# A two-sequence decoder layer rewritten: token-major residual, two halves of 512 tokens per pass, norms and attention placed between dense matmuls

## The chip, the cores and the metric

The kernel runs as one program on the eight cores of one Trainium2 chip. Each core has the same weights and two of the sixteen prompt sequences, with four of the 32 sample rows. The cores do not exchange data. The metric is the device time of the slowest core in microseconds.

Executions come in two states. In the fast one all cores agree within about 1%; in the slow one the cores of one die (0 to 3 or 4 to 7), sometimes of both, run longer at a lower mean clock.

In the profiles PE is TensorE (PEld its weight loads), DVE is VectorE, ACT is ScalarE, POOL is GpSimd and SP is SyncE; a name with a q (POOLq, SPq) is the part of an engine that issues DMAs. The granted clock is the share of its full rate at which TensorE ran. A mixer is the stage between the two FFNs: projections, pooling, attention, gates and output. Residue order for a step of 4 or 16 means that tokens with the same remainder lie side by side.

## The reference, cut to what matters

Per layer, with 1024 channels, sequences of 2048 tokens and a hidden width of 2816:

```python
x = x + 0.5 * swiglu(rmsnorm(x, norm_ffn1), ffn1_gate, ffn1_up, ffn1_down)
h = rmsnorm(x, norm_mix)
z = h @ w_in            # u (512) | 3 groups x (q, k, v) x 4 heads x 64 | gate_pool | gate_attn
pool = pool_mix(u)      # trailing means over 2, 4, 8, 16 tokens, a linear map per 128 channels
attn = 3 groups of causal windows (128, step 1), (512, step 4), (2048, step 16), rotary q and k,
       merged by their softmax denominators
x = x + (sigmoid(gate_pool) * (pool @ w_pool_br) + sigmoid(gate_attn) * (attn @ w_attn_br)) @ w_o
x = x + 0.5 * swiglu(rmsnorm(x, norm_ffn2), ffn2_gate, ffn2_up, ffn2_down)
y = rmsnorm(x, norm_final)
```

The outputs are y, the last pooling rows, and the key and value windows of the prompt; and the same for the sample rows. The sample rows' windows are cache rows shifted by one: about 22 MB per core that are only copied from one place in DRAM to another.

## The kernel before

One pass takes 512 tokens, so a core makes eight passes. The residual x is kept with channels on the partitions (`xT`). Each stage is its own block: norm, FFN, mixer, norm, FFN, final norm. Norms square all of x on ACT and DVE, average over the partitions with a matmul against a constant, and only then scale:

```python
def norm(gi, seg, out_f32=None, next_func=None):
    for c in range(8):
        if c % 2 == 0:  act: hT[:, c] = Square(xT[:, c])
        else:           dve: hT[:, c] = xT[:, c] * xT[:, c]
    K.mmg(b, [(ps[b][:, 0:n], meanm[:], hT_[:, c, 0:n], {"rd": [hT_.r[c]]}) for c in range(8)], ...)
    act: rstd = Exp(-0.5 * Ln(ps + EPS))
    for c in range(8):  dve: hT[:, c] = xT[:, c] * gains[c] * rstd
```

(shortened; the first and last lines of its loops stand for whole calls.) Rotated keys of the two groups with steps 4 and 16 are put into residue order by ACT copies that write with a stride (the normed x is copied in the same way before the values are projected):

```python
if g == 1:
    return [(kT1[:, ab, base:base + 512].rearrange("p (r i) -> p i r", r=4), slice(0, T))]
v = kT2[:, ab, :].rearrange("p (r m) -> p m r", r=16)
...
act.op(lambda dst=dst, src=src: nc.scalar.copy(out=dst, in_=src), reads=[kf.r[ab_]], writes=kres)
```

Weights are fp32 in DRAM. In the first pass a software DMA casts each tile and writes a bf16 copy back; later passes read the copy, once for each 512 tokens:

```python
def wload(first_pass, slot, slot_ap, src_f32, scr_ap, scr_res, sem3, arena_bound):
    if first_pass:
        ...
        pool.dma(slot_ap, src_f32, sem3[0], writes=slot.r)
        sp.dma(scr_ap, slot_ap, sem3[1], reads=slot.r, writes=[scr_res])
    else:
        ...
        sp.dma(slot_ap, scr_ap, sem3[2], reads=[scr_res], writes=slot.r)
```

The softmax here doesn't subtract the row's maximum and nothing guards it: scores larger than these inputs give would overflow.

## Time and profile before

4201.22 us, median of three runs (4198.58 to 4201.73).

| | before |
|---|---|
| passes 0 to 7, us | 790, 474, 485, 518, 471, 472, 474, 479 |
| the same in pairs (two passes, 1024 tokens) | 1264, 1003, 943, 953 |
| TensorE busy | 3484.7 us, 83% |
| read from HBM | 481.65 MB |

A pass length is the distance between two ends of the final norm in the chain of waits. Of the page of the kernel before, here are the busy time (us, share, instructions), TensorE's busy tenths in forty equal slices, and the granted TensorE clock in tenths in the same slices:

```profile
PE 3484.7 (83%) x19775; PEld 1817.0 (43%) x19775; DVE 1314.8 (31%) x2151; ACT 1016.3 (24%) x1625; POOL 247.4 (6%) x287
...
PE   1857875898997889867898879988898979987898
...
PEclk6977687997798969988799987999799987998799
```

The dips in the last two lines come together: where TensorE waits, its clock halves too. There is one such dip every four or five slices, one a pass (a slice is 105 us). 83% busy therefore overstates what TensorE does: matmuls at half clock are counted as busy for twice as long.

### The profile page before, as it was taken

Reading aid. Unit: us, or ns where it says so; the run is one execution under the profiler, and the core shown is the slowest. Engines: PE = TensorE matmul, PEld = TensorE weight load, DVE = VectorE, ACT = ScalarE, POOL = GpSimd, SP = SyncE. Lnnn points to the kernel's source line nnn. Section 1 sums busy time; section 2 is a strip of 40 time slices with the busy share of each in tenths; the row PEclk is TensorE's granted clock in tenths of the full one; section 3 lists DMA queues with packets and bytes.
Section 4 is the critical chain, followed back from the end, with each engine's and each line's share of the span. In section 5 each row is a group of like instructions: output and inputs, shape, how many; then the busy total and the mean of one; then the engine's idle time right before and its main releaser. Section 6 shows DMA issues by size and latency. Waiting matters only on the chain.

```text
span 4186.3 us, 55101 instructions; the slowest of 8 cores (4148.3 to 4186.3 us)
## 1 busy us (share of the span) xinstructions
PE 3484.7 (83%) x19775; PEld 1817.0 (43%) x19775; DVE 1314.8 (31%) x2151; ACT 1016.3 (24%) x1625; POOL 247.4 (6%) x287
## 2 busy tenths in 40 slices
PE   1857875898997889867898879988898979987898
PEld 0325532445543364433644345443644445443643
DVE  1125130325313333314333153134333162233432
ACT  1123220214211232112421142122321152122321
POOL 1100020002000020000200001000200010000200
PEclk6977687997798969988799987999799987998799
DMA  7963199531436206382164614452063423542151
GB/s 131 204 140 65 40 201 201 151 113 60 149 121 184 93 14 210 115 192 71 38 204 129 160 58 128 147 167 91 21 206 120 135 63 109 161 146 85 37 180 58
DMA packets 210535, 512.59 MB, mean 122 GB/s; under 512 B 19038, under 2 KB 116598, under 8 KB 200668
## 3 DMA queue, kind: packets, MB, share of 16 engines
q1 hardware_dynamic: 108512, 413.49, 31.3%
q0 software_dynamic: 101760, 95.58, 14.8%
q8 instruction: 166, 2.72, 0.3%
q14 instruction: 97, 0.79, 0.1%
HBM read 481.65 MB, written 98.24 MB: 139 GB/s over the span
## 4 chain that ended last, share of the span: by engine, by line
PE 68%; DMA 9%; DVE 7%; ACT 7%; issue 5%; another core or an unknown queue 3%; DVEq 0%; SPq 0%; POOL 0%; ACTq 0%; POOLq 0%
PE ps L190 60%; PE ps L896 4%; ACT sb_mergedT L203 3%; PE ps L188 2%; DMA sb_w_29<-wu 2%; DMA sb_w_28<-wscr 2%; PE ps L922 1%; DVE sb_xT L427 1%; DVE sb_hT L423 1%; DVE sb_qT L554 1%; DMA sb_w_33<-wu 1%; DMA sb_w_31<-wu 1%; DVE sb_hT L411 1%; DMA sb_w_28<-wg 1%
## 5 line engine op out<-in xcount | busy, mean ns | idle before, releaser
L190 PE MATMUL ps<-sb_hT,sb_w_30 128*128 128x512 bf16 x1152 | 304.8, 403 | 64.2 <-ACT sb_uext L662 36.1
L190 PE MATMUL ps<-sb_hT,sb_w_28 128*128 128x512 bf16 x768 | 210.4, 411 | 135.8 <-DMA sb_w_28<-wscr 58.2
L190 PE MATMUL ps<-sb_hT,sb_w_34 128*128 128x512 bf16 x1024 | 278.6, 412 | 26.6 <-DVE sb_hT L423 19.5
L190 PE MATMUL ps<-sb_hT,sb_w_31 128*128 128x512 bf16 x1152 | 285.6, 394 | 10.7 <-DMA sb_w_31<-wu 8.2
L190 PE MATMUL ps<-sb_hT,sb_w_35 128*128 128x512 bf16 x1024 | 242.9, 381 | 6.7 <-DMA sb_w_35<-wu 6.6
L190 PE MATMUL ps<-sb_hT,sb_w_29 128*128 128x512 bf16 x768 | 197.8, 406 | 57.2 <-DMA sb_w_29<-wu 57.2
L190 PE MATMUL ps<-sb_hT,sb_w_33 128*128 128x512 bf16 x896 | 212.5, 382 | 5.6 <-DMA sb_w_33<-wu 5.6
L190 PEld LDWEIGHTS ps<-sb_hT,sb_w_30 128*128 128x128 bf16 x1152 | 114.7, 101 | 232.7 <-issue 117.9
L190 PE MATMUL ps<-sb_hT,sb_w_32 128*128 128x512 bf16 x896 | 212.7, 382 | 2.3 <-DVE sb_rtmp_53 L556 2.3
L495 DVE SCALAR_TENSOR_TENSOR sb_xT<-ps,sb_xT 128x512 f32<-128x512 f32 x96 | 66.4, 691 | 403.7 <-PE ps L190 403.7
L190 PEld LDWEIGHTS ps<-sb_hT,sb_w_28 128*128 128x128 bf16 x768 | 77.3, 102 | 250.8 <-issue 177.7
L190 PEld LDWEIGHTS ps<-sb_hT,sb_w_31 128*128 128x128 bf16 x1152 | 115.4, 101 | 156.4 <-issue 30.3
L190 PEld LDWEIGHTS ps<-sb_hT,sb_w_34 128*128 128x128 bf16 x1024 | 103.0, 103 | 178.9 <-issue 81.5
L203 ACT COPY sb_mergedT<-sb_hT 128x512 bf16<-128x512 bf16 x64 | 158.9, 2482 | 50.5 <-DVE sb_hT L423 45.6
L423 DVE SCALAR_TENSOR_TENSOR sb_hT<-sb_xT,sb_gains,sb_rstd 128x512 bf16<-128x512 f32 x192 | 129.3, 746 | 93.4 <-ACT sb_rstd L417 93.4
L190 PEld LDWEIGHTS ps<-sb_hT,sb_w_35 128*128 128x128 bf16 x1024 | 100.5, 99 | 130.9 <-issue 14.0
L190 PE MATMUL ps<-sb_hT,sb_meanm 128*128 128x512 bf16 x256 | 88.6, 454 | 77.7 <-DVE sb_hT L411 48.8
L190 PEld LDWEIGHTS ps<-sb_hT,sb_w_29 128*128 128x128 bf16 x768 | 78.7, 103 | 160.6 <-issue 81.7
L405 ACT ACT_TABLE_LOAD x26 | 33.4, 1283 | 467.8 <-DVE sb_xT L495 280.1
L190 PEld LDWEIGHTS ps<-sb_hT,sb_w_33 128*128 128x128 bf16 x896 | 87.9, 99 | 112.9 <-issue 10.2
L408 ACT ACTIVATE sb_hT<-sb_xT 128x512 bf16<-128x512 f32 x128 | 72.3, 618 | 256.0 <-DVE sb_xT L495 158.6
L190 PEld LDWEIGHTS ps<-sb_hT,sb_w_32 128*128 128x128 bf16 x896 | 86.9, 98 | 105.9 <-issue 4.2
(997 smaller groups left out, 5267.2 us busy)
## 6 DMA issues: line engine op xcount, KB each, us to landing
sb_w_30<-wscr SPq DMA_DIRECT2D x63, 512.0 KB, 3.9
sb_w_31<-wscr SPq DMA_DIRECT2D x63, 512.0 KB, 4.5
sb_w_34<-wscr SPq DMA_DIRECT2D x63, 512.0 KB, 3.9
sb_w_35<-wscr SPq DMA_DIRECT2D x63, 512.0 KB, 4.5
sb_w_28<-wscr SPq DMA_DIRECT2D x49, 512.0 KB, 4.0
sb_w_29<-wscr SPq DMA_DIRECT2D x49, 512.0 KB, 5.2
sb_w_32<-wscr SPq DMA_DIRECT2D x49, 512.0 KB, 3.9
sb_w_33<-wscr SPq DMA_DIRECT2D x49, 512.0 KB, 4.7
```

Of the source, the lines that this page charges most:

```text
L188: fn = lambda o=o, l=l, r=r: self.nc.tensor.transpose(o, l, r)
L190: fn = lambda o=o, l=l, r=r, st=st, sp_=sp_, kw=kw: self.nc.tensor.matmul(o, l, r, start=st, stop=sp_, **kw)
L203: return eng.op(lambda: self.nc.scalar.copy(out=out, in_=in_), reads, writes)
L405: act.op(lambda: nc.scalar.activation(out=dummy[:, 0:1], in_=dummy[:, 2:3], func=AF.Ln))
L408: act.op(lambda c=c: nc.scalar.activation(out=hT_[:, c, 0:n], in_=xT_[:, c, 0:n], func=AF.Square), reads=[xT_.r[c]], writes=[hT_.r[c]])
L411: dve.op(lambda c=c: nc.vector.tensor_tensor(out=hT_[:, c, 0:n], in0=xT_[:, c, 0:n], in1=xT_[:, c, 0:n], op=ALU.mult), reads=[xT_.r[c]], w ...
L423: dve.op(lambda c=c: nc.vector.scalar_tensor_tensor(out=hT_[:, c, 0:n], in0=xT_[:, c, 0:n], scalar=gains[:, gi, c:c + 1], in1=rstd_[:, 0:n ...
L427: dve.op(lambda c=c: nc.vector.scalar_tensor_tensor(out=xT_[:, c, 0:n], in0=xT_[:, c, 0:n], scalar=gains[:, gi, c:c + 1], in1=rstd_[:, 0:n ...
L495: dve.op(lambda b=b, m=m, n=n, xT_=xT_: nc.vector.scalar_tensor_tensor(out=xT_[:, m, 0:n], in0=ps[b][:, 0:n], scalar=0.5, in1=xT_[:, m, 0: ...
L554: dve.op(lambda: nc.vector.tensor_tensor(out=outA, in0=view(t[0][:, 0:n]), in1=view(t[1][:, 0:n]), op=ALU.subtract), reads=t[0].r + t[1].r ...
L896: pe.op(lambda outap=outap, lhsT=lhsT, pb=pb, u_=u_: nc.tensor.matmul(outap, lhsT, pb[:, u_ * 128:(u_ + 1) * 128], start=False, stop=False ...
L922: pe.op(lambda outap=outap, lhsT=lhsT, pb=pb, r=r, h=h: nc.tensor.matmul(outap, lhsT, pb[0:kr, r * 32:(r + 1) * 32], start=False, stop=Fal ...
```

## The change

The kernel is rewritten as a whole; this is its core. Two halves A and B of 512 tokens make a pair, so there are four passes. The residual is token-major, so a norm's statistic is a sum along a row, which one ACT instruction gives as a by-product, and GpSimd makes the power of -1/2 from it:

```diff
-            b = K.bank()
-            K.mmg(b, [(ps[b][:, 0:n], meanm[:], hT_[:, c, 0:n], {"rd": [hT_.r[c]]}) for c in range(8)], reads=meanm.r)
...
+            act.op(lambda: nc.scalar.activation(out=junk[0:n, :], in_=xap, func=AF.Square, scale=1.0 / 32, accum_out=st[:, 0:1]),
+                   reads=xres, writes=r + junk.r)
+            pool.op(lambda: nc.gpsimd.tensor_scalar(st[:, 1:2], st[:, 0:1], 1.0, EPS, op0=ALU.mult, op1=ALU.add), reads=r, writes=r)
+            pool.op(lambda: nc.gpsimd.tensor_tensor(out=st[:, 2:3], in0=st[:, 1:2], in1=mhalf[0:n, :], op=ALU.pow),
+                    reads=r + mhalf.r, writes=r)
```

The scaling and the transposes of a block are tasks that are put off by some us of counted TensorE time and come up between dense groups (`K.later`, `K.pump`). In the FFNs one fetch of a weight tile serves both halves, half B two tiles behind half A, and the hidden width is cut in three parts, each with its own part of the down projection. There are seven slots for weight tiles:

```diff
+PARTS = ((0, 3), (3, 7), (7, 11))
+NSLOT = 7
+LAG = 2
...
+                for (h, jp) in order:
+                    if h == 0:
+                        held[jp] = (wget("wg%d" % f, jp), wget("wu%d" % f, jp))
+                    wg, wu = held[jp]
```

In the mixer, attention of one half is a list of small steps that fills in among dense groups: A's among B's projections, B's among A's gates. Sigmoid becomes tanh. Group 2's values go through DRAM to be put in residue order (`v2scr`).

```diff
+            run([dn[0], uA[0], dn[1], uA[1]])
+            K.banks = DN
+            run(dn[2:5] + [uA[2]] + dn[5:8] + [uA[3]] + dn[8:], [lambda: K.flush(before=mk)] + attn_thunks(A), tail=1)
...
+            run(gate_groups(A) + u_groups(B) + wA[:4] + pm + wA[4:], [lambda: K.flush(before=mk2)] + attn_thunks(B), first=4, tail=3)
```

The cache copies stay as large as they were, but come at other places: none in pair 0, then two at the start of a mixer and three before FFN 2:

```diff
+            ffn(0, LAG if pr else 1, lambda h, b: norm_blk(h, b, 1))
+            copies(2 if pr else 0)
...
+            load_gain(3, sp)
+            copies(3 if pr else 0)
```

## The prediction

> **What bounds the kernel now.** I first read the table of cores: spans of 4148 to 4186 us and mean clocks of 0.860 to 0.867, so no core or die is the odd one. The clock records of all cores hold only two values, full and half. Then the chain that ended last: 68% TensorE and 9% DMA, so TensorE's order sets the end, but a third of the chain is not matmul. The chain in order of time gives the pass borders (the final norm's DVE line ends each pass): 790 us for pass 0, then 474, 485, 518, 471, 472, 474 and 479. Cutting one steady pass at the chain's stage borders gives, from the windows view (start:end, length, busy us and instructions per engine, granted clock, DMA share, GB/s):
>
> ```profile
> 2766.00:2880.00 114.00, 113.81 (x521) 51.12 (x519) 19.89 (x30) 13.14 (x22) 0.00 (x0) 0.99 0.53 149
> 2880.00:3011.95 131.95, 107.37 (x757) 73.03 (x758) 66.67 (x100) 58.91 (x79) 21.56 (x23) 0.75 0.17 51
> 3011.95:3020.46 8.51, 4.88 (x97) 4.77 (x97) 1.80 (x3) 2.93 (x5) 0.00 (x0) 0.50 0.01 2
> 3020.46:3076.00 55.54, 55.08 (x244) 24.29 (x244) 20.65 (x31) 13.48 (x21) 0.00 (x0) 0.96 0.54 158
> 3076.00:3090.00 14.00, 7.30 (x16) 1.90 (x17) 8.48 (x13) 6.27 (x10) 0.00 (x0) 0.74 0.99 310
> 3090.00:3204.00 114.00, 114.00 (x522) 51.30 (x521) 19.97 (x29) 17.14 (x28) 0.00 (x0) 0.99 0.42 132
> 3204.00:3237.00 33.00, 18.94 (x89) 11.60 (x88) 21.81 (x33) 10.81 (x19) 1.83 (x3) 0.84 0.40 127
> ```
>
> The two FFNs (first and sixth line) are already at the limit: 521 matmuls of 512 columns in 114 us is 219 ns each, at clock 0.99, on this core, while the other cores I asked do the same. Gates and output (fourth line) are nearly so. Everything else, 131.95 + 8.51 + 14 + 33 = 187 us of 471, is norms, projections, attention, input and output transposes, done one after another: TensorE there waits for DVE and ACT, and at clock 0.50 in the last part of attention. Why the second line is long shows in the groups by shape: copies that write with a stride are four times as slow as the plain ones below them.
>
> ```profile
> L203 ACT COPY sb_mergedT<-sb_hT 128x512 bf16<-128x512 bf16 x64 | 158.9, 2482 | 50.5 <-DVE sb_hT L423 45.6
> L737 ACT CAST sb_kT_20<-sb_kf 128x512 bf16<-128x512 f32 x16 | 41.1, 2566 | 0.7
> L203 ACT COPY sb_ystage<-ps 128x512 f32<-128x512 f32 x32 | 18.8, 587 | 76.3 <-PE ps L188 39.6 <-DVE sb_ystage L204 36.7
> ```
>
> Pass 0 is another regime. In the chain (start, length, what) it stands for weights:
>
> ```profile
> 54.18 49.50 DMA sb_w_29<-wu
> ...
> 113.89 33.11 DMA sb_w_29<-wu
> ...
> 163.97 33.45 DMA sb_w_31<-wu
> ...
> 224.54 27.70 DMA sb_wd_42<-wd
> ...
> 572.65 32.05 DMA sb_w_28<-wg
> ```
>
> There fp32 weights are cast by software DMA and written back as bf16. FFN 2 of pass 0 needs 33 tiles of 512 KB and lasts from 540 to 785 us: 7.4 us a tile.
>
> **What the skill says.** (1) The Trainium skill, "TensorE: Matmul & The Clock Gate", Part 1, has the clock at half after an idle window of about 3.4 us, and a warm matmul at N/2.4 GHz plus 2.5 ns, 215.7 ns for 512 columns. The trace agrees: 219 ns including the cold start, and half clock in attention. (2) The same part says that the clock drops to 13/16 within 5 to 20 us once three cores of a die are dense. This trace does not show it: eight cores, 114 us dense, 0.99. I follow the trace, but keep the possibility open for millisecond-long density. (3) "ScalarE: Activation LUTs", Table sets: exp and tanh share a set, ln and exp share another[...]. The trace has 1283 ns loads, ahead of Ln, Silu and Sigmoid. The change's tanh in place of sigmoid can therefore run amid attention's exp without a load. (4) "DMA: Bandwidth & Descriptors", Specifications, wants at least 512 B for line rate. Pass 0 casts 256-column slices, 512 B a row, just at that edge: 204 GB/s counted at 1.18 DMA share between 105 and 210 us, against 310 GB/s at 0.99 in the fifth line above.
>
> **The change, part by part.** Dense work is unchanged. Per 512 tokens: FFNs 2 x 528, u 32, q/k 96, V 48 (as 512 columns), gates and branches 176, output 64: 1472 matmuls of 215.7 ns = 318 us, eight times 2540 us. It is the floor.
>
> Extra TensorE work per 512 tokens in the new kernel, counted from its loops:
> - Three norms of 4 blocks x 8 transposes of 128 columns, 96 x 0.06 us (2.5 ns + 128/2.4 GHz) = 5.5 us. They replace 4 x 8 mean matmuls (6.9 us) and all fp32 transposes of x and y (64 x 116 ns = 7.4 us), since the residual stays token-major.
> - Permuting q/k transposes, 48 x 0.06 = 3 us. They replace the strided ACT and DVE copies: one pass's 8 ACT permutations alone are 20 us.
> - Attention with two heads zero-padded to 128 rows, and values and ones in one stationary: 20 score steps and their value matmuls, about 9.5 us for groups 0 and 1, and 96 small matmuls of 0.06 us for group 2, 13 us in all. The old one ran from 2963 to 3017, about 54 us, mostly at half clock.
> - Pool map, 4 matmuls, 1 us.
>
> So 341 us per 512 tokens, 682 for a pair of halves, 2728 for four pairs, if TensorE never waits.
>
> The waits. Norms now trail by block behind down projections or the other half's work, so the 14 and 33 us holes should vanish; each half's attention is woven into the other's projections or its gates, so the clock should stay full. Weights are read once per pair in the FFNs, again per half in the mixer: 118 tiles x 0.52 MB = 62 MB in 682 us, 91 GB/s, below the 120 GB/s of now.
>
> Other engines, per half. ACT: 44 silu x 0.6, 16 squares and 12 transposed evictions of 1024 columns at about 1.1, 16 tanh, 20 exp, about 90 small evictions at 0.3: 115 us. DVE: 44 products, 56 residual adds and 32 rope products near 0.69, gates 16, 16 norm scales at 1.25, masks 12 and merges 6: about 145 us. POOL: rope adds and pooling chains (1.06 us per 526 columns), about 60. All are under half of 341. Locally they are tighter: in the two attention stretches (about 38 and 73 us of TensorE) dense groups have only three PSUM banks, and I find ACT at 85% of the first. The four pooling chains of half B take POOL 20 us against about 19 us of matmuls before their result is used, with the norm statistics queued behind. Weight slots (7) force some waits of 2 to 4 us where four output tiles follow the gates. I put all such waits at 5% to 6% of the pair, about 40 us: 722 us each.
>
> Pair 0 has more. Its 92 tiles first come as fp32: at the old 7.4 us they take 681 us, about the compute of a pair, but now each serves two halves, and rows of 2048 contiguous columns should go faster. Unevenly: the first projections want 9 tiles in 34 us and gate and output 15 in 73. I allow 30 us. The sample rows add about 1400 tiny matmuls, 85 us, and 30 us of serial chains. Before the first FFN matmul all eight blocks of x must arrive and be normed: 45 us. So 722 + 30 + 115 + 45 = 912 us, against 790 + 474 now for the same tokens.
>
> Sum: 912 + 3 x 722 + 10 for the last stores = 3088 us; with 4% of waits it would be 3040. I take 3060, 1140 us less: about 350 from pass 0, the rest from some 115 us in each of seven passes (471 - 357).
>
> **Rivals.**
> - *Power takes it back.* The new kernel is dense for 3 ms rather than 114 us at a time. If the clock fell to 13/16 throughout, 2728 would become 3360 and the whole some 3700 us. For: the skill's sentence, and the fact that eight cores were never dense longer than an FFN. Against: no value between half and full in any core's records. About one in ten.
> - *The weave is bound by evictions.* [...]with three banks, one late statistic from POOL or a slow strided merge (DVE reading PSUM by stride; the trace has only strided writes, 1.85 us for 512) stalls TensorE, and the clock may fall. If the mixer ran at 70% of its 214 us per pair rather than near 85%, that is 305 us against 250 and the total some 3280 us. The old mixer's DVE and ACT are half idle, which speaks against a whole-kernel bound, not against local ones.
> - *Pair 0 stays DMA-bound.* If fp32 tiles came no faster and each stage waited, it would lose 100 us more: 3160 us.
> - *No waits at all:* 2728 + 85 + 45 + 10 = 2870 us. The FFN stretches of now, 1% above the warm rate, show that it can be neared.
>
> **Range and chances.** The floor of 2870 and the eviction rival at 3280 bracket the answer; only the power rival leaves it upward, and even that is over 10% faster than now. Range 2920 to 3270. Faster by over 2%: 0.98; within 2%: 0.01; slower: 0.01.
>
> **What would show it.** Mean clock above 0.95 on every core; TensorE busy over 92% in steady pairs of about 720 us; FFN stretches at 216 to 220 ns a matmul; mixer near 250 us per pair with only short waits, for DVE or POOL; pair 0 near 900 us; no ACT copy over 1.3 us. Wrong would be: a clock of 0.8 in dense stretches (power), TensorE waits on ACT or DVE over 60 us a pair (evictions), or pair 0 over 1000 us on weight transfers.

## More of the kernel before

The cache copies (4 of 4 MB, 4 of 1 MB, some small ones) are queued after the second pass, and the program has one issued after each FFN stage. In the trace GpSimd gets to them at the starts of passes: one at 1277 us, two at 1762, two at 2281, and so on.

```python
def issue_copy(nmax=1):
    for _ in range(nmax):
        if K.pending_copies:
            dst, src = K.pending_copies.pop(0)
            (sp if K.pass_idx == 0 else pool).dma(dst, src, ds_misc)
```

## The result, and the profile after

3195.53 us, median of five runs: 3193.53, 3194.76, 3195.53, 3482.81 and 3560.46. The ratio to the kernel before is 0.7605 (95% interval 0.7592 to 0.7618). Ratios here are the mean time of one kernel's fast runs over that of the other's fast runs of the same rounds, so they are not quite the ratio of the medians.

The lines of the page of the kernel after that answer to those above, with the row of the cache copies from its list of DMA issues (KB each, median us from issue to landing):

```profile
PE 2819.9 (88%) x15566; PEld 1366.5 (43%) x15857; DVE 1224.0 (38%) x1881; ACT 909.6 (28%) x1946; POOL 415.3 (13%) x754
...
PE   4999578899999937887899998889999999888998
...
PEclk9999789999999978998899999999999999999999
...
kvs<-c POOLq DMA_DIRECT2D x4, 4094.0 KB, 45.8
```

A slice is 80 us here. The regular dips are gone. What is left is the start, a dip in the first mixer (slices 5 and 6), and two in the middle (slices 15, 16 and 19), in the second pair, where the clock dips as well. The second half of the kernel has none.

The order of TensorE's instructions is fixed, so the start of each stage can be counted off in the trace. On the slowest core (start of pair 0 at 55.2 us; all in us):

```
                         pair 0   pair 1   pair 2   pair 3
both FFNs                 502.3    505.5    463.8    462.0
  of it FFN 2, first down  22.7     58.6     20.7     20.7
mixer                     338.0    317.1    266.8    273.6
  of it A's projections   100.5     92.5     53.0     44.8
whole pair                840.3    822.6    730.6    735.6
```

The windows view of the kernel after, in the columns of the first fence of the prediction (start:end, length; busy us and instructions of PE, PEld, DVE, ACT and POOL; granted clock, DMA share, GB/s). First the start; then A's projections and FFN 2's first down stage in pair 1; then one whole FFN, the five mixer stages (A's projections, B's projections with A's attention, B's queries and last keys, A's gates and output with B's attention, B's gates and output) and the first parts of FFN 2 in pair 2; last A's projections in pair 3:

```profile
3.20:55.20 52.00, 9.16 (x73) 7.28 (x73) 30.77 (x21) 17.68 (x25) 10.62 (x23) 1.00 1.01 249
...
1131.90:1224.40 92.50, 37.91 (x225) 20.32 (x228) 20.07 (x32) 22.87 (x80) 20.98 (x38) 0.70 0.76 168
1491.80:1550.40 58.60, 24.30 (x95) 9.73 (x96) 10.36 (x15) 0.35 (x1) 0.00 (x0) 0.68 0.69 171
...
1718.00:1950.00 232.00, 230.37 (x1105) 106.95 (x1126) 76.98 (x105) 47.80 (x76) 9.76 (x24) 1.00 0.31 104
1950.60:2003.60 53.00, 37.45 (x226) 20.06 (x229) 20.04 (x31) 23.19 (x82) 21.02 (x38) 0.87 0.57 174
2003.60:2047.70 44.10, 35.69 (x290) 20.71 (x292) 23.26 (x45) 28.10 (x83) 28.61 (x42) 0.96 0.41 142
2047.70:2064.60 16.90, 15.94 (x88) 7.93 (x89) 11.17 (x18) 8.81 (x28) 9.19 (x16) 1.00 0.40 125
2064.60:2161.80 97.20, 76.36 (x462) 38.44 (x470) 46.01 (x72) 47.85 (x101) 27.69 (x40) 0.90 0.26 86
2161.80:2217.30 55.50, 53.95 (x267) 25.24 (x272) 26.55 (x36) 18.73 (x29) 2.41 (x7) 1.00 0.42 143
2217.30:2448.40 231.10, 229.94 (x1092) 106.41 (x1113) 76.80 (x105) 47.41 (x76) 13.16 (x26) 1.00 0.37 116
...
2680.90:2725.80 44.90, 38.42 (x226) 20.47 (x229) 20.09 (x32) 22.95 (x80) 20.97 (x38) 0.92 0.49 170
```

An FFN of two halves keeps TensorE busy for 230 of 232 us at clock 1.00. The old one did this too, but lost 33 and 14 us at its edges; here norms, final norm and input loads lie inside. The mixer stages reach 71% to 97%. The line to stop at is the second: 228 weight loads for the same matmuls as in the last line, in 92.5 us in place of 44.9, with DMA engines busy 76% of the time, yet moving only 168 GB/s. The third line is like it: 96 weight loads that take 20.7 us elsewhere.

So, by difference of stage starts: pair 0 with its start fell from 1264 to 895 us, pair 1 by 180, pair 2 by 212, pair 3 by 217, the end from 23 to 10. That is 991 us, the difference of the two profiled spans (4186.3 and 3194.5).

Where pair 1 stood is told by the waits view of the kernel after between 1125 and 1225 us (who waited for whom: us in total, times, longest us):

```profile
POOL qkb_98 L895 <- DVE tB_138 L886: 64.3, 3, 62.6
DVE vf_104 L989 <- ACT vst_81 L911: 57.4, 2, 56.1
...
ACT vst_81 L911 <- DMA v2scr<-vst_81: 55.8, 1, 55.8
PE ps L279 <- POOL qkb_98 L895: 53.7, 1, 53.7
```

Read it from the line of ACT. ACT must empty the next block of values into a staging buffer, of which there are two, and waits 55.8 us until the store of that buffer's earlier content to DRAM has landed. ACT runs nothing else meanwhile, so DVE waits for ACT, GpSimd for DVE, and TensorE for GpSimd: four engines stand still for one store of 96 KB. The windows view shows it, with no instruction on DVE, ACT or GpSimd for 52 us and DMA engines at 99% (TensorE ends its last 6.3 us of work at the start of it):

```profile
1142.00:1194.00 52.00, 6.29 (x35) 2.89 (x34) 0.00 (x0) 0.00 (x0) 0.00 (x0) 0.59 0.99 182
```

The DMA view of that stage (2 stores, KB each, median us to landing) and of the same stage of pair 3:

```profile
kvs<-c POOLq DMA_DIRECT2D x2, 4094.0 KB, 45.0
...
v2scr<-vst_81 SPq DMA_DIRECT2D x2, 96.0 KB, 30.0
...
v2scr<-vst_81 SPq DMA_DIRECT2D x2, 96.0 KB, 6.0
```

In pair 3 no copy of 4 MB is under way, only two of 254 KB. The median of two, 30.0, hides one store of 58.2 us beside one of under 2, and the 6.0 one of 10.4 beside one of 1.6. The same first store of the stage took 58.2, 19.1 and 10.4 us in pairs 1, 2 and 3, where the two copies issued just before it are of 4 MB, 1 MB and 254 KB, and 7.9 us in pair 1 of the run without copies (e11): it follows the size of the copies. The chain of waits (start, length, what) has these as its long pieces; the first two are in pair 0:

```profile
533.41 15.93 DMA w_66<-wt
...
643.96 20.11 DMA w_65<-wt
...
1139.52 55.76 another core or an unknown queue
...
1479.34 49.80 DMA w_66<-wscr
```

Two waits of 16 and 20 us for fp32 tiles are what is left of the weight waits of pass 0. The other two begin just where copies are issued, before the mixer and before FFN 2. The third, which the chain puts down to an unknown queue, is the store of the waits view. The fourth is a weight tile behind three copies.

### The profile page after: what moved, and what is told of

It is laid out like the page before. It is cut to its first block, busy times and chain, and to the rows that moved or that the text cites. A ratio compares the mean times of both kernels' runs of the same rounds, so it can differ in the third digit from the quotient of the medians.

```text
span 3194.5 us, 47060 instructions; the slowest of 8 cores (3163.4 to 3194.5 us)
## 1 busy us (share of the span) xinstructions
PE 2819.9 (88%) x15566; PEld 1366.5 (43%) x15857; DVE 1224.0 (38%) x1881; ACT 909.6 (28%) x1946; POOL 415.3 (13%) x754
## 4 chain that ended last, share of the span: by engine, by line
PE 76%; DMA 7%; ACT 5%; issue 4%; DVE 4%; another core or an unknown queue 2%; POOL 1%; SPq 0%; ACTq 0%; DVEq 0%; POOLq 0%
PE ps L269 74%; DMA w_66<-wscr 2%; DMA v2scr<-vst_81 1%; DMA x_46<-x 1%; PE ps L279 1%; PE ps L580 1%; DMA w_65<-wt 1%; ACT qz_56 L911 1%; ACT poolT L1251 1%; DMA w_66<-wt 0%; SPq L149 0%; DMA w_63<-wscr 0%; ACT qz_57 L911 0%; DMA kvp<-vf_105 0%
## 5 line engine op out<-in xcount | busy, mean ns | idle before, releaser
L568 POOL TENSOR_SCALAR stat<-stat 128x1 f32<-128x1 f32 x128 | 35.0, 273 | 1748.4 <-ACT junk L566 1738.3
L831 ACT ACTIVATE st_110<-ps 128x512 f32<-128x512 f32 x88 | 52.5, 596 | 663.7 <-PE ps L269 663.7
L269 PE MATMUL ps<-hT_48,w_65 128*128 128x512 bf16 x572 | 139.5, 384 | 3.8 <-ACT qz_58 L911 1.7
L834 DVE TENSOR_TENSOR act_109<-st_112,ps 128x512 bf16<-128x512 f32 x79 | 54.3, 687 | 224.7 <-PE ps L269 224.7
L269 PE MATMUL ps<-hT_48,w_64 128*128 128x512 bf16 x561 | 136.9, 385 | 3.8 <-ACT qz_58 L911 2.9
L834 DVE TENSOR_TENSOR act_108<-st_110,ps 128x512 bf16<-128x512 f32 x79 | 54.3, 687 | 222.8 <-PE ps L269 208.5
L834 DVE TENSOR_TENSOR act_109<-st_113,ps 128x512 bf16<-128x512 f32 x79 | 54.3, 687 | 218.9 <-PE ps L269 218.9
L834 DVE TENSOR_TENSOR act_108<-st_111,ps 128x512 bf16<-128x512 f32 x79 | 54.3, 687 | 217.4 <-PE ps L269 217.4
L269 PE MATMUL ps<-hT_48,w_63 128*128 128x512 bf16 x543 | 133.1, 385 | 3.1 <-ACT qz_58 L911 1.7
L269 PE MATMUL ps<-hT_49,w_65 128*128 128x512 bf16 x549 | 131.5, 379 | 3.5 <-DMA w_65<-wscr 2.9
L269 PE MATMUL ps<-hT_49,w_64 128*128 128x512 bf16 x547 | 131.1, 379 | 1.6 <-DMA w_64<-wscr 0.8
L269 PE MATMUL ps<-hT_49,w_63 128*128 128x512 bf16 x528 | 127.2, 379 | 1.7 <-DMA w_63<-wscr 0.8
L831 ACT ACTIVATE st_112<-ps 128x512 f32<-128x512 f32 x88 | 52.6, 598 | 245.3 <-PE ps L269 245.3
L831 ACT ACTIVATE st_113<-ps 128x512 f32<-128x512 f32 x88 | 52.6, 598 | 239.3 <-PE ps L269 239.3
L831 ACT ACTIVATE st_111<-ps 128x512 f32<-128x512 f32 x88 | 52.6, 598 | 237.6 <-PE ps L269 237.4
L269 PE MATMUL ps<-hT_49,w_69 128*128 128x512 bf16 x502 | 119.6, 379 | 0.6
L269 PE MATMUL ps<-hT_48,w_69 128*128 128x512 bf16 x439 | 106.7, 383 | 11.2 <-ACT kT_52 L911 6.4
L858 DVE SCALAR_TENSOR_TENSOR x_43<-ps,x_43 128x512 f32<-128x512 f32 x96 | 66.4, 691 | 125.4 <-PE ps L269 125.4
L269 PE MATMUL ps<-hT_48,w_68 128*128 128x512 bf16 x442 | 107.3, 386 | 1.1 <-DMA w_68<-wt 0.8
L269 PE MATMUL ps<-hT_49,w_67 128*128 128x512 bf16 x433 | 104.9, 379 | 0.8
L269 PE MATMUL ps<-hT_49,w_68 128*128 128x512 bf16 x442 | 105.0, 379 | 0.3
L269 PE MATMUL ps<-hT_48,w_67 128*128 128x512 bf16 x433 | 103.6, 379 | 0.9
```

Source lines behind the costliest of these rows:

```text
L269: self.pe.op(lambda o=o, l=l, r=r, kw=kw: self.nc.tensor.matmul(o, l, r, **kw), reads=rds, writes=[self.psr[bank]] if i == 0 else (), inc= ...
L568: pool.op(lambda: nc.gpsimd.tensor_scalar(st[:, 1:2], st[:, 0:1], 1.0, EPS, op0=ALU.mult, op1=ALU.add), reads=r, writes=r)
L831: act.op(lambda: nc.scalar.activation(out=st[:, :], in_=ps[bg][:, :], func=AF.Silu), reads=[psr[bg]], writes=st.r)
L834: dve.op(lambda: nc.vector.tensor_tensor(out=actb[h][:, jl, :], in0=st[:, :], in1=ps[bu][:, :], op=ALU.mult), reads=st.r + [psr[bu]], writ ...
L858: dve.op(lambda: nc.vector.scalar_tensor_tensor(out=xap, in0=ps[bk][:, :], scalar=0.5, in1=xap, op0=ALU.mult, op1=ALU.add), reads=[psr[bk] ...
```

## The experiments

Eleven kernels ran; each is the kernel after with one edit unless said otherwise. All are correct except the one that leaves out outputs. My theory after reading the traces: the copies of the decode cache, of which the prediction does not say a word, cost pair 1 some 90 us. At first I took the size of their packets to be the reason, and had as a rival that their bytes fill the DMA engines in front of small stores and weight tiles; after e1 the rival became the theory. Other rivals: that the stage's own transfers are slow and the copies a coincidence; and that the bytes cost the same wherever they go. Besides, I tested four other terms of the sum: sharing tiles, the weave, the start, and the fp32 tiles.

### Copies in rows of 4 KB, at the same place (e1_rows4k)

In the trace of the kernel after, the copies go in packets of 65504 bytes, of 5886 ns each, beside packets of 4 KB of 212 ns (means between 1125 and 1225 us). The Trainium skill, "DMA: Bandwidth & Descriptors", Queues, rings and completion order, says that each DMA engine goes round its queues and drains a whole packet before it switches. If so, smaller packets should let the stores through.

```diff
-                    a = 16 if nel % 16 == 0 else 1
+                    a = nel // (Lg - 1)
```

(and each copy in two halves, so that it can be split over the engines.)

> The cache copies are issued in the same places with the same bytes, but cut into rows of about 4 KB that cannot be joined, in place of packets of 65504 bytes. Theory (every other transfer waits behind one 65504-byte packet, 5.9 us, at each turn): the first projections of pair 1 fall from 92 us to under 60, down part 0 of its second FFN from 59 us to under 30, and the whole from 3195 to 3100-3130 us. Rival (the copies' bytes fill the DMA for some 46 us, whatever the packets): both stretches stay above 80 and 50 us, the whole at 3180-3200 us. Second rival (pair 1 is long for another reason): no change.

Measured: 3218.97 us, four fast runs of 3210.70 to 3224.07, ratio 0.7666 (0.7637 to 0.7694). A's projections in pair 1 took 96.0 us, FFN 2's first down stage 58.8. The DMA view between 1125 and 1225 us:

```profile
kvs<-c POOLq DMA_DIRECT2D x2, 2048.0 KB, 51.2
kvs<-c POOLq DMA_DIRECT2D x2, 2046.0 KB, 62.9
...
v2scr<-vst SPq DMA_DIRECT2D x4, 96.0 KB, 19.2
```

The packets were 4 to 8 KB now, 460 and 754 ns on average. No store waited 58 us any more, but three in a row took 33, 22 and 17, and the stage was no shorter. The whole was 24 us slower than the kernel after, which none of the three expectations has; pairs 2 and 3 grew by 9 and 3. The packet theory falls as far as it is about the sizes in the trace: the stage lasts as long as the copies have bytes in front of it. (The page counts several descriptors, 9 to 17 as a rule, to a packet; whether a record of the trace is such a packet or one descriptor, no view says, so at which sizes the engines switched stays open.)

### Copies in 262 KB pieces through both FFNs (e2_pieces)

```diff
-                    a = 16 if nel % 16 == 0 else 1
-                    src = cache_d[g][bb, 1:Lg, :, :].rearrange("r t f -> (r t f)").rearrange("(a c) -> a c", a=a)
-                    dst = kvs_d[g][bb, 0:Lg - 1, :, :].rearrange("r t f -> (r t f)").rearrange("(a c) -> a c", a=a)
-                    pend_copy.append((dst, src))
+                    npc = {2: 16, 1: 4, 0: 1}[g]
+                    fl = lambda t_: t_.rearrange("r t f -> (r t f)").rearrange("(n a c) -> n a c", n=npc, a=16)
+                    src, dst = fl(cache_d[g][bb, 1:Lg, :, :]), fl(kvs_d[g][bb, 0:Lg - 1, :, :])
+                    for q_ in range(npc):
+                        pend_copy.append((dst[q_], src[q_]))
...
+                    if h == 0 and not K.pass0:
+                        copies(1)
...
+                        if b % 2 == 0 and not K.pass0:
+                            copies(1)
...
-            copies(2 if pr else 0)
...
-            copies(3 if pr else 0)
```

> The same copies cut into pieces of 262 KB (packets of 16 KB), one piece at a time spread over the FFNs of pairs 1 to 3, none in a mixer. Theory: pair 1 falls from 823 to 730-740 us, like pairs 2 and 3, and the whole to 3090-3110 us. If pair 1 is long for another reason than the copies, it stays above 800 us.

Measured: 3141.27, 3143.02 and 3143.80 us, ratio 0.7485 (0.7453 to 0.7518). A's projections fell to 38.3, 38.5 and 41.0 us in pairs 1 to 3. But first down stages rose from 20.7 to between 27.6 and 41.6 us in four of six FFNs. So the copies do cost the mixer its time, and half of the cost went to another place: a gain of about 52 us and not 95.

### Pieces in the second and third part of the FFNs only (e9_pieces2)

```diff
+                    if h == 0 and pi and not K.pass0:
+                        copies(2)
```

(in place of the two calls of `copies(1)` above.)

> The pieces of 262 KB again, but only in the second and third part of each FFN, two at each weight pair, where five of seven slots are free to run ahead; none in the first part, where six slots are held. Theory after the first four runs (a copy costs as long as its bytes fill the DMA and something waits in series for a transfer, whatever the packets): the stalls of the first down parts (14 to 21 us each in four places) go, every stage of pair 1 is as in pair 3, the whole 3095-3115 us. Rival (the bytes must be paid somewhere): 3140 us as with the pieces everywhere.

Measured: 3128.39, 3132.37 and 3132.87 us fast (four slow ones), ratio 0.7445 (0.7429 to 0.7462). FFN 2's first down stage was back at 20.7 to 21.4 us, FFN 1's was not: 29.0, 32.5, 33.4, and the whole is nearer to the rival's 3140 than to the theory's 3095 to 3115. FFN 1's stage is odd, since no piece stands before it in the program. The trace shows why: a piece waits for nothing, and GpSimd has little to do in an FFN, so it ran ahead of TensorE and issued all sixteen pieces of FFN 1 in pair 1 within 7.3 us, from 915.9 to 923.2, long before the parts in which I had written them. The next run tests this reading.

### The same pieces, each held until TensorE's latest group is done (e10_paced)

```diff
                     dst, src = pend_copy.pop(0)
+                    pool.wait_tok((pe.sem, pe.cnt))
                     pool.dma(dst, src, ds_misc)
```

> As the previous version with the cache copies in 262 KB pieces in parts 2 and 3 of the FFNs, but GpSimd waits for TensorE's latest matmul group before it issues each piece, so that the pieces really come two per weight pair (about every 14 us) and not sixteen at once (in the trace of the unpaced run GpSimd issued all sixteen of an FFN between 915.9 and 923.2 us, and the last landed 32 us later). Theory (the bunch fills the queues in front of weight tiles): the first down stage falls from 29-33 us back to about 21 in pairs 1 to 3, the first FFN stage of the next half is as without copies, and the whole is 3085 to 3115 us, ratio about 0.738. Rival (it is the bytes of the copies beside the weight stream wherever they are, or GpSimd's waits delay norm statistics): 3125 to 3150 us, as unpaced.

Measured: five fast runs from 3095.04 to 3097.38 us, ratio 0.7363 (0.7346 to 0.7381), as the theory has it. The DMA view from 900 us on, over the first stages of FFN 1 of pair 1, first unpaced (e9, to 990 us):

```profile
w<-wscr SPq DMA_DIRECT2D x9, 512.0 KB, 15.8
...
kvs<-c POOLq DMA_DIRECT2D x16, 255.9 KB, 21.9
```

and paced (to 1000 us):

```profile
w<-wscr SPq DMA_DIRECT2D x13, 512.0 KB, 4.2
...
kvs<-c POOLq DMA_DIRECT2D x4, 255.9 KB, 5.0
```

Sixteen pieces at once made weight tiles land after 15.8 us; four that come apart leave them at 4.2. The windows view of the paced kernel, for the first down stage of FFN 1, A's projections and the first down stage of FFN 2 in pair 1:

```profile
950.20:970.90 20.70, 20.70 (x97) 9.41 (x96) 10.36 (x15) 0.34 (x1) 0.00 (x0) 1.00 0.17 51
1138.90:1177.30 38.40, 35.93 (x229) 19.48 (x228) 20.07 (x32) 22.79 (x80) 19.82 (x36) 1.00 0.53 186
1444.90:1465.60 20.70, 20.70 (x98) 9.39 (x97) 10.37 (x15) 0.29 (x1) 0.00 (x0) 1.00 0.15 51
```

The stages of 92.5 and 58.6 us are now 38.4 and 20.7, at clock 1.00. The pairs take 843.7, 732.9, 721.4 and 729.2 us.

### No copies at all (e11_nocopy)

The cache copies are dropped and their output rows never written, so this kernel's result is wrong.

```diff
-                    dst, src = pend_copy.pop(0)
-                    pool.dma(dst, src, ds_misc)
+                    pend_copy.pop(0)
```

> Wrong on purpose: the changed kernel without the decode-cache copies (the rest of the copied cache rows is never written). It measures by itself what these transfers cost. Theory (they cost pair 1 about 90 us and pair 2 about 10): pair 1 falls from 823 to about 730, pairs 2 and 3 stay at 725 to 736, pair 0 stays at 840, and the whole is 3085 to 3105 us. Rival (the stalls come from the loads of the mixer's own weights and the stores of this stage, and the copies only coincide): 3150 us or more, with the first projection stage of pair 1 still above 70 us.

Measured: four fast runs of 3096.10 to 3098.33 us, ratio 0.7365 (0.7348 to 0.7383); pairs of 843.9, 735.0, 720.1 and 731.8. This is the cost of the copies measured by itself: about 97 us in the kernel after (3195 less 3098, runs on different chips; by the ratios (0.7605 - 0.7365) x 4200 = 101 us), 88 of them in pair 1, 10 in pair 2, 4 in pair 3. A's projections of pair 1 fell to some 39 us, so the stage's own stores and loads are not at fault by themselves. And the paced kernel, which does all the copying, is no slower than this one: placed so, 22 MB cost nothing that these runs can show.

### Tiles fetched once per half, not shared (e3_refetch)

```diff
-                    if h == 0:
-                        held[jp] = (wget("wg%d" % f, jp), wget("wu%d" % f, jp))
-                    wg, wu = held[jp]
+                    wg, wu = wget("wg%d" % f, jp), wget("wu%d" % f, jp)
```

(and the same for the down tiles, with the slots given back after each half.)

> In the FFNs each half fetches its own weight tiles: the sharing of tiles by the two halves is undone, the first (fp32) fetch is still only one in the program. Theory (a tile lands in about 4 us and is used for 8.4 us by one half, so sharing buys nothing on the steady path): within 1% of 3195 us, the steady FFNs still at 231 us, about 35 MB more read per pair. Rival (sharing is what keeps TensorE fed): FFNs of 250 us or more, the whole over 3300 us.

Measured: 3316.98 and 3317.29 us fast (three slow), ratio 0.7901 (0.7867 to 0.7935): 122 us slower where I had expected hardly anything. The pairs grew by 58, 32, 24 and 14 us. The waits view of TensorE has this row first (in the kernel after the rows of this kind, one for each buffer, sum to 41.8 us):

```profile
PE ps L269 <- DMA w<-wscr: 134.9, 41, 31.0
```

The waits lie in the down stages of four tiles: the last one of an FFN rose from 29.4 to 41.2 us in pair 2. That fits a simple account, which I have not tested: four of the seven slots are in use by half A, so when half B wants the same four tiles again, only three can be on their way. If it holds, sharing matters for the slots as well as for the bytes, also in the steady pairs, where the prediction counts bytes alone.

### Attention by itself, not woven in (e4_noweave)

```diff
-            run([dn[0], uA[0], dn[1], uA[1]])
+            run([dn[0], uA[0], dn[1], uA[1]] + dn[2:5] + [uA[2]] + dn[5:8] + [uA[3]] + dn[8:])
+            K.flush()
             K.banks = DN
-            run(dn[2:5] + [uA[2]] + dn[5:8] + [uA[3]] + dn[8:], [lambda: K.flush(before=mk)] + attn_thunks(A), tail=1)
+            run([], attn_thunks(A))
```

(and likewise for half B, ahead of A's gates.)

> Attention of each half runs by itself instead of amid dense groups; the dense groups then have all eight PSUM banks. Theory (attention alone is bound by ACT's exponentials and the chain score, exponential, mask, value, about 25-30 us per half, against some 13 us of TensorE work when woven): 12-18 us more per half, 3290-3340 us, with half clock in the attention stretches. Rival (the weave only moves the wait for evictions into the dense groups): 3195 plus or minus 30 us.

Measured: four fast runs of 3235.79 to 3248.28 us, ratio 0.7727 (0.7699 to 0.7754), so 50 us slower, a third to a half of what I had expected. The stage of B's projections with A's attention in pair 1 took 67.6 us rather than 51.6. The windows view of most of that stretch:

```profile
1228.00:1290.00 62.00, 39.93 (x259) 21.92 (x260) 17.98 (x39) 28.84 (x84) 30.39 (x50) 0.83 0.41 132
```

Clock 0.83 (0.80 over the whole stage) rather than 0.89: the clock falls in the stretch of small matmuls, but far less than in the old attention, at 0.50. Over eight halves the weave is worth some 6 us each. Most of the gain over the old attention, which took about 54 us a pass in the prediction's reading, is in the attention's own form (two heads padded to 128 rows, values and ones in one tile), not in where it stands: by itself, half A's attention of pair 2 in this run took 24 us, from 2049.5 to 2073.6. This is argued from the runs; I did not run the old form in the new place.

### Three edits that moved a wait and not the end

**B's u projections ahead among A's gates (e5_ubearly)**, so that the pooling chains on GpSimd are over before norm statistics queue behind them:

```diff
+            gA, uB = gate_groups(A), u_groups(B)
-            run(gate_groups(A) + u_groups(B) + wA[:4] + pm + wA[4:], [...
+            run(gA[:8] + uB[:2] + gA[8:12] + uB[2:] + gA[12:] + wA[:4] + pm + wA[4:], [...
```

> Half B's four pooling groups move from after half A's gates to amid them, so that GpSimd's pooling chains (about 20 us) are done before the norm statistics of the output stage are queued on it. Theory (DVE waits some 4 us for a statistic behind the chains, and TensorE for DVE): the stage with half A's gates shortens by 4 to 8 us in each of four pairs, the whole to 3165-3185 us. Rival (the same evictions only move): within 8 us of 3195.

Measured: 3192.96 us, five fast runs of 3181.29 to 3199.53, ratio 0.7592 (0.7571 to 0.7613). The stage fell from 100.4, 97.2 and 100.7 to 98.9, 92.6 and 98.6 us in pairs 1 to 3, but rose by 11 in pair 0. No gain in all, as the rival has it.

**Only half A normed before the first matmul (e6_start)**:

```diff
-        for h in range(2):
-            for b in range(4):
-                norm_blk(h, b, 0, d1=0.0, d2=0.0)
+        for b in range(4):
+            norm_blk(0, b, 0, d1=0.0, d2=0.0)
...
+        for b in range(4):
+            K.later(1.0 + 1.5 * b, lambda b=b: norm_blk(1, b, 0, d1=1.0, d2=2.0))
```

> Only half A is normed before the first FFN matmul; half B's four blocks follow amid the first groups. Theory (the first matmul waits for all eight blocks of x, 36 us): first FFN matmul at 35-42 us instead of 55, the whole 10-18 us shorter, 3177-3185 us. Rival (the first weight tiles or half B's x are late anyway): under 5 us.

Measured: 3185.10, 3189.95 and 3195.19 us fast, ratio 0.7585 (0.7565 to 0.7605). The first FFN matmul came at 49.8 us rather than 55.2, but the first part of the FFN ended at 103.0 rather than 100.9. The first line of the windows fence of the kernel after tells why: DMA share 1.01 over the whole start. There, x, the gain row and the first fp32 tiles share the DMA engines (half B's x landed from 36 to 47 us in both kernels), and the order of norms does not bring them earlier.

**The fp32 tiles in rows of 512 bytes, as the old kernel reads them (e7_rows512)**:

```diff
-                    pool.dma(slot[:, :], wt_d[ti, :, :], wsem[s][0], writes=slot.r)
+                    pool.wait_deps([], slot.r)
+                    pv = lambda t_, o: t_.rearrange("p (k c) -> p k c", c=256)[:, o:8:2, :]
+                    nc.gpsimd.dma_start(out=pv(slot[:, :], 0), in_=pv(wt_d[ti, :, :], 0)).then_inc(wsem[s][0].sem, 16)
+                    wsem[s][0].total += 16
+                    pool.dma(pv(slot[:, :], 1), pv(wt_d[ti, :, :], 1), wsem[s][0], writes=slot.r)
```

> The fp32 tiles of pair 0 are fetched in rows of 256 columns (512 bytes as bf16) instead of 2048, as the kernel before did. Theory (the rows made the cast faster than 7.4 us a tile, and sharing alone would leave pair 0 DMA-bound in its mixer): pair 0 rises from 840 to 890-960 us, all else the same, 3245-3315 us. Rival (sharing each tile between two halves is all that mattered): pair 0 within 15 us of 840.

Measured: 3184.81 to 3193.52 us in four fast runs, ratio 0.7581 (0.7566 to 0.7597). Pair 0 took 852.4 us from a start at 42.5, so it ended at 895 us as before. Between 105 and 210 us there were 13138 packets of 512 B at 73 ns for 6.73 MB, against 1607 of 4096 B at 435 ns for 6.58 MB. That is 959 us of engine time against 699, so the large rows are better for the DMA engines, but the end of pair 0 does not move with them. The start did: half B's x landed at 24 to 30 us here, rather than at 36 to 47 behind the first weight tiles, and the first matmul came some 13 us earlier on every core; pair 0 lost them again. I have not looked for the reason.

### Paced pieces, and B's u projections ahead in pairs 1 to 3 only (e12_both)

```diff
+            gu = gA[:8] + uB[:2] + gA[8:12] + uB[2:] + gA[12:] if pr else gA + uB
```

(with the edits of e9 and e10.)

> The paced pieces together with half B's u-projection groups moved ahead among half A's gates, in pairs 1 to 3 only (pair 0 lost 11 us by it, the others gained 1.5 to 4.6). If the two parts add: 3 to 10 us below the paced version of the same rounds, 3080 to 3110 us; if they do not, within 3 us of it.

Measured: 3082.70, 3086.76, 3087.24 and 3088.79 us fast, two slow, ratio 0.7339 (0.7322 to 0.7357), against 3095.04 to 3097.38 of the paced kernel in the same rounds. So the two parts add, by 10 us. This version beats the kernel after by 3.5% (0.7339 over 0.7605).

## Why the prediction was right or wrong, point by point

The direction and the range were right: 3195 lies in 2920 to 3270, 4.4% above the 3060 given. That the range held is in part luck: its upper end stands for the rival of evictions, which did not come, and the copies took up that room. Term by term against the sum of 3088:

```
                predicted   measured   off     without the copies (e11)
start               45        55       +10        56
pair 0             867       840       -27       844
pair 1             722       823      +101       735
pair 2             722       731        +9       720
pair 3             722       736       +14       732
end                 10        10         0        10
sum               3088      3195      +107      3097
```

(Pair 0 is the 912 us of the prediction without its start of 45.)

**The step that failed** is the sentence on waits: "I put all such waits at 5% to 6% of the pair, about 40 us: 722 us each." It lists waits for evictions, norm statistics and weight slots, and no transfer that is not a weight. The copies of the decode cache were in view: the diff has their calls, and the profile before has passes 2 and 3 at 485 and 518 us, where passes 6 and 7, at the same places of the other sequence, take 474 and 479. The prediction quotes these lengths and does not ask why they differ. The first copies of 4 MB are issued at the starts of passes 2, 3 and 4, and the old chain has a wait of 32, 33 and 37 us soon after each (pass 4, which starts a sequence, is no longer than the others for it; its attention has fewer earlier keys to take in, which may hide the wait). The prediction should have taken a copy at what the old trace shows, 50.5 us from issue to landing for the first, and asked which transfer the next stage cannot do without. In the old kernel these waits are for weight tiles (two by the chain, the third by the waits view); in the new one it is first a store of 96 KB that holds up ACT. By the lengths of passes 2 and 3, the old kernel lost 11 and 39 us to copies there; by e11 the new one loses about 100 in all.

With that term taken out, 722 was good: 735, 720 and 732 in e11 and 733, 721 and 729 in the paced kernel. The last step, from 3088 to 3060 "with 4% of waits", had nothing behind it, and the other 28 us of the miss are there.

**Dense work at the floor**: right. FFNs of two halves take 463 us a pair in pairs 2 and 3; 4 x 528 matmuls of 215.7 ns are 456. The "219 ns" that the prediction read off was too high: it divides by the 521 records of a trace that misses some (528 matmuls were issued), and the distance from one matmul to the next is 215.8 ns in both kernels.

**Clock**: right in the fast state, but for one core of eight. The prediction asked for a mean over 0.95 on every core; the cores show 0.948 to 0.955, and 0.964 and 0.965 at the lowest in the paced kernel and in e11. The power rival did not come in the fast runs; two of the five runs of the kernel after were slow ones at some 3500 us, which I do not explain.

**Mixer near 250 us a pair, evictions no bound**: right in kind, 8 to 17 us low. Without copies in the way it takes 258 to 267 us in pairs 2 and 3 (paced kernel). The waits are those foretold: a scaling of the norm waits 3.97 us for a statistic of GpSimd behind the pooling chains, and TensorE waits up to 5.3 us for the last block after B's attention. In all TensorE waits 46 us in pair 2: 16.6 for GpSimd, 14.6 for ACT, 13.7 for DVE and 1.1 for DMAs. That is near the 40 put down, and the 28 for ACT and DVE are well under the 60 that were to speak for evictions. No ACT copy is longer than 1.08 us, where the old kernel's strided ones took 2.5.

**TensorE over 92% busy in steady pairs**: right, 680.3 of 730.4 us and 688.75 of 735.6, 93% and 94%.

**Pair 0**: right in its sum (840 against 867), for partly wrong reasons. It is 110 to 120 us longer than the other pairs, which have no sample rows (paced kernel): 40 in the FFNs and some 80 in the mixer, of which A's projections alone are 60. How much of it the sample rows cost, no run shows: the chain there has three waits of 9.60, 10.42 and 9.38 us for small stores issued while fp32 tiles are under way, the same kind of wait as behind the copies. The DMA-bound rival, 100 us more, did not come. The "7.4 us a tile" is misread: at 540 us the old chain still waits for a tile of `w_o`, FFN 2's first tile is asked for at 552.5 and its last lands at 767.6, which is 6.5 us for each of the 33. "Rows of 2048 contiguous columns should go faster" is not what helped, by e7. That each tile now serves two halves did: giving it up costs pair 0 58 us (e3, where half B reads the bf16 copy again; the fp32 fetch is still a single one).

**Start**: 55 against 45. The prediction counts the arrival of x and the norms, and not the fp32 tiles that share the DMA engines, at a share of 1.01; an earlier first matmul (49.8 us in e6, 42.5 in e7) did not bring pair 0's end forward.

**What the parts of the rewrite are worth**: sharing tiles in the FFNs 122 us and the weave 50, of about 1000, each by taking it out of the kernel after. What the rest divides into (norms inside the FFNs, no strided copies, the attention's form) I have not measured apart.

## What to carry to other kernels

Count the transfers that nobody computes with. A copy from DRAM to DRAM has no consumer in the chain, so no view of waits names it (the list of DMA issues does); it shows as a small store or a weight tile that lands ten times later than its neighbours, and as long passes in which such a copy is under way. Cut it into pieces, put them where the DMA share is low, and tie each piece to the progress of the busiest engine: an engine with nothing to wait for issues its DMAs long before the place where they stand in the program.

## What the Trainium skill lacked or had wrong

- "DMA: Bandwidth & Descriptors" has no figure for what a large copy from DRAM to DRAM does to other transfers. Here, on one DMA engine, such a copy moved 65504 B in 5886 ns, 11.1 B/ns, where the 4 KB packets of loads and stores took 193 ns on average over the run, 21.2 B/ns; while two copies of 4 MB were under way, a store of 96 KB took 58.2 us, rather than 7.9 without copies, and with sixteen pieces of 256 KB queued at once a weight tile took 15.8 us rather than 4.2.
- The same page, Queues, rings and completion order, has the engines change queues at each packet. No run here contradicts it, but it doesn't say how its packets, of several descriptors, relate to the records of a trace, and no gain followed: records of 4 to 8 KB in place of 64 KB left the stage as long as it was (96.0 against 92.5 us).
- "TensorE: Matmul & The Clock Gate", Part 1, has the 13/16 clock within 5 to 20 us once three cores of a die are dense. In the profiled fast run of a kernel that is dense on eight cores for 3 ms it is the exception: six cores have records of 0.5 and 1.0 only, cores 6 and 7 have 0.812 for 96 and 103 us; the profiles of the eleven experiments have none. Slow runs have a die at a mean of 0.82 (cores 4 to 7 in one run of e12, at 3520.65 us).
- "SBUF — State Buffer", Who interferes with whom, has a DVE instruction with two SBUF inputs contend with a GpSimd instruction that reads SBUF. The trace agrees: the attention's mask product (128 x 512) took 0.42 us alone, and 0.85 us in the median and up to 1.51 us when GpSimd was at work beside it, the slowest beside its pooling chain. The page has ratios of other measurements, and none for this pair.
- I found no page with the cost of a power on GpSimd: 570 ns on average for 128 x 1, and 273 ns for the multiply and add ahead of it, a latency that each of the 128 norm statistics pays.
